# The down projection's accumulators move from SBUF to DRAM: ACT copies each finished tile out of PSUM and a DMA adds it to an array in DRAM

## The chip, the core and the metric

The kernel runs on one core of one Trainium2 chip. Each engine executes its own instructions in order: TensorE (PE) multiplies, VectorE (DVE) and ScalarE (ACT) do elementwise work and read PSUM, GpSimd (POOL) does elementwise work and can issue DMAs, SyncE (SP) issues most DMAs here. The metric is the device time of one execution in microseconds; lower is better.

## The reference, cut to what matters

The layer is a token-mixing block (attention heads beside a recurrent group) followed by an MLP. The change lies in the MLP alone, which is, for 512 tokens, D = 2048 and FF = 8192, all in float32:

```python
h = _rmsnorm(x, pre_mlp_g) * (1.0 + scale_m) + shift_m
y = jnp.square(jax.nn.relu(h @ w_up)) @ w_down
x = x + gate_m * _rmsnorm(y, post_mlp_g)
```

## The kernel before, in words

**Precision.** Each float32 operand is split into a high and a low part (`hl`: a CAST on ACT writes the high part, a TENSOR_TENSOR subtract on DVE the low part), and each product is three matmuls (high by high, high by low, low by high).

**Groups and rounds.** FF is cut into 16 groups of 512. While PE does the down projection of group g (steps "D"), it also does the up projection of group g+1 (steps "U"). The string `ROUND` writes this order out by hand: 22 steps, 14 of them D (12 matmuls each) and 8 U (24 matmuls each). There are 15 such rounds; `FIRST` is the order of the first. After them `down_last` does the down projection of the last group, token tile by token tile (128 tokens at a time), adds it to the sums, norms the row and stores it.

**Seven products.** The down projection of one group for one of two column sets c (512 columns of each half of D) is a Strassen-like scheme: seven products f = 0 to 6 instead of eight. Each writes a PSUM tile `dn` of 128 x 1024 (two token tiles by 512 columns). There are two such tiles, and f = 2, 3, 6 go on in the tile of f = 0, 1, 4. So a product can start only when the tile has been read that was written two products earlier. `product` (line 1194) issues the 12 matmuls (L1207 to L1209) and then adds the tile to its place: f = 0 and 5 to `V`, the other five to parts of `y`, an SBUF tile of 4 token tiles by 2048 columns (32 KB a partition). The addition is one DVE TENSOR_TENSOR (L1218); in the first group ACT copies instead where nothing is there yet (L1216). In the last round `add_V` (L1246) adds `V` to three parts of `y`.

**What orders the work.** The order on each engine is fixed when the program is built. `ahead` runs the weight preparation two steps ahead of PE. Weights come through SP's queue: `w_up` into `raw` tiles, `w_down` into `B` tiles (five of them, also used for `lraw`, the last group's `w_down`, and for `x2r`, the residual rows that `down_last` reads back). From the second round to the sixth, `interleave` adds one unit of the modulation's gate to each U step (its weights are read from `w_mod` through the same `raw` tiles). At the end of a round `hidden` (ACT's Relu into `u`, DVE's square) and `make_forms` (CASTs `fH`, subtracts `fL`) prepare the next group's operands.

Of the kernel before, what the change touches and what calls it, by code (L numbers as in the profile page):

```python
# [10 lines left out]
F32 = mybir.dt.float32  # L11
# [4 lines left out]
ALU = mybir.AluOpType  # L16
# [4 lines left out]
P = 128  # L21
S = 512
NT = S // P
D = 2048
# [28 lines left out]
def encoder_layer(ctx: ExitStack, tc: tile.TileContext, a, out):  # L53
    nc = tc.nc

    def pool(name, bufs=1, **kw):
        return tc.tile_pool(name=name, bufs=bufs, reuse_waits="tile", **kw)
# [18 lines left out]
    dram = ctx.enter_context(pool("dram", space=DRAM))  # L76
# [2 lines left out]
    w_mod, w_in, w_uq, w_ukv = a["w_mod"][0], a["w_in"][0], a["w_uq"][0], a["w_ukv"][0]  # L79
    w_out, w_up, w_down = a["w_out"][0], a["w_up"][0], a["w_down"][0]  # L80
    x2_d = dram.tile([S, D], F32, name="x2_d")

    def mmt(name):
        return banks["mm"].tile([P, 512], F32, tag="mm", name=name)
# [142 lines left out]
    def mm3(o, s_h, s_l, m_h, m_l, first, last):  # L227
        nc.tensor.matmul(o, s_h, m_h, start=first, stop=False)  # L228
        nc.tensor.matmul(o, s_h, m_l, start=False, stop=False)  # L229
        nc.tensor.matmul(o, s_l, m_h, start=False, stop=last)  # L230
# [5 lines left out]
    def rstd(r, ss, n):  # L236
        nc.scalar.activation(r, ss, AF.Sqrt, bias=eps[:, 0:1], scale=1.0 / n)
        nc.vector.reciprocal(r, r)
# [84 lines left out]
    with ExitStack() as ph:  # L323
# [385 lines left out]
        for gid, w, rate in ((("kv", 0), 256, RATE["kv"]), (("ql", 0), 512, RATE["ql"])):  # L709
            pss = run_block(gid, 0, KD, units, PER[gid[0]], steps, rate)  # L710
            if w == 256:
                t4 = v_tile()
                dst = [t4[:, t, :] for t in range(NT)]
            else:
                t2 = [z_tile(), z_tile()]
                dst = [t2[t // 2][:, t % 2, :] for t in range(NT)]
# [44 lines left out]
    for i in range(2):  # L761
        c = 2 * 2048 + 1024 * i
# [3 lines left out]
    with ExitStack() as ph:  # L766
# [66 lines left out]
        for k0 in range(0, 4, 2):  # L833
            src = w_uq[k0 * P:(k0 + 2) * P, :].rearrange("(k p) (h c) -> p k h c", p=P, c=192)
# [196 lines left out]

    with ExitStack() as ph:
        ml = ph.enter_context(pool("ml"))
        y = ml.tile([P, NT, D], F32, name="y")
        V = ml.tile([P, 2, 1024], F32, name="V")
        G = ml.tile([P, D], F32, name="G")
        NG = FF // 512
# [2 lines left out]
        def btile(name):  # L1040
            return ml.tile([P, 1024], F32, tag="B", name=name, bufs=NB)

        def ubank(n):
            return banks["up"].tile([P, 512], F32, tag="up", name=f"up{n}")

        def dset(name):
            return banks["dn"].tile([P, 1024], F32, tag="dn", name=name)
# [30 lines left out]
        for i in range(2):  # L1078
            c = 5 * 2048 + 1024 * i
# [114 lines left out]
        def product(q, fm, H, L):  # L1194
            s, f = divmod(q, 7)
            g, c = divmod(s, 2)
            fH, fL = fm[FORMS[f]]
            goes_on = {2: 0, 3: 1, 6: 4}.get(f)
            X = sets[f] = sets.pop(goes_on) if goes_on is not None else dset(f"dn{f}")
            for t in range(2):  # L1200
                o = X[:, 512 * t:512 * t + 512]
                ts_ = slice(t * P, (t + 1) * P)
                for k in range(2):
                    first, last = k == 0 and goes_on is None, k == 1
                    sh, sl, mh, ml_ = fH[:, k, ts_], fL[:, k, ts_], H[:, k, :], L[:, k, :]
                    skip = goes_on is not None
                    nc.tensor.matmul(o, sh, mh, start=first, stop=False, skip_group_check=skip)  # L1207
                    nc.tensor.matmul(o, sh, ml_, start=False, stop=False, skip_group_check=skip)  # L1208
                    nc.tensor.matmul(o, sl, mh, start=False, stop=last, skip_group_check=skip)  # L1209
            cs = slice(512 * c, 512 * c + 512)  # L1210
            c2 = slice(1024 + 512 * c, 1024 + 512 * c + 512)
            dst, fresh = [(V[:, :, cs], True), (y[:, 2:4, c2], True), (y[:, 0:2, cs], True), (y[:, 0:2, c2], True),
                          (y[:, 2:4, c2], False), (V[:, :, cs], False), (y[:, 2:4, cs], True)][f]
            Xv = X.rearrange("p (t n) -> p t n", t=2)
            if g == 0 and fresh:
                nc.scalar.copy(dst, Xv)  # L1216
            else:
                nc.vector.tensor_tensor(dst, dst, Xv, ALU.add)  # L1218


        VSIGN = {(0, 1): ALU.add, (2, 0): ALU.add, (2, 1): ALU.add}
        held = []

        def hold(g):
# [16 lines left out]
            return uu  # L1241

        def add_V(c, t0, t1, j):
            cs = slice(512 * c, 512 * c + 512)
            o = y[:, t0:t1, 1024 * j + 512 * c:1024 * j + 512 * c + 512]
            nc.vector.tensor_tensor(o, o, V[:, :, cs], VSIGN[t0, j])  # L1246

        def down_last(uu):
            for t in range(NT):
                ts_ = slice(t * P, (t + 1) * P)  # L1250
                xr = [btile(f"x2r{h}") for h in range(2)]
                for h in range(2):
                    nc.sync.dma_start(xr[h], x2_d[t * P:(t + 1) * P, 1024 * h:1024 * h + 1024])
                r = small.tile([P, 6], F32, tag="r6", name="r6")
                for c in range(4):
                    cs = slice(512 * c, 512 * c + 512)
                    ps = ubank(f"l{t}")
                    for k in range(4):
                        H, L = held[2 * c + k // 2]
                        mm3(ps, uu[k][0][:, ts_], uu[k][1][:, ts_], H[:, k % 2, :], L[:, k % 2, :], k == 0, k == 3)  # L1260
                    yv = y[:, t, cs]
                    nc.vector.tensor_tensor(yv, yv, ps, ALU.add)
                    jk = stream.tile([P, 1024], F32, tag="raw", name="yjk", bufs=4)[:, 0:512]
                    nc.scalar.activation(jk, yv, AF.Square, accum_out=r[:, 1 + c:2 + c])
                    nc.vector.tensor_tensor(yv, yv, G[:, cs], ALU.mult)
                nc.vector.reduce_sum(r[:, 0:1], r[:, 1:5], axis=AX.X)
                rstd(r[:, 0:1], r[:, 0:1], D)
                for c in range(4):
                    cs = slice(512 * c, 512 * c + 512)
                    nc.vector.scalar_tensor_tensor(y[:, t, cs], y[:, t, cs], r[:, 0:1],  # L1270
                                                   xr[c // 2][:, 512 * (c % 2):512 * (c % 2) + 512], ALU.mult, ALU.add)
                    nc.sync.dma_start(out[t * P:(t + 1) * P, cs], y[:, t, cs])


        pss = [mmt(f"up{n}") for n in range(4)]
# [26 lines left out]
        n = 0  # L1302
        for g in range(NG - 1):
            fm = make_forms(u if g == 0 else hidden(pss))
            pss = [ubank(i) for i in range(4)]
            for _ in range(22):
                ahead(n + 1 + LEAD)
                what, _, i = steps[n]
                H, L = wts.pop(n)
                if what == "U":  # L1310
                    up_mms(pss, i, H, L, 0, NT)
                    if g == NG - 2:
                        if i >= 8:
                            hold(NG - 1)
                        if i == KD - 2:
                            uu = last_forms(pss)
                    elif g > 0:
                        interleave(units, 1)
                else:
                    product(i, fm, H, L)  # L1320
                    if g == NG - 2:
                        c, f = divmod(i % 14, 7)
                        done[c].add(ORDER[f])
                        for need, t0, t1, j in (({5, 4}, 2, 4, 1), ({5, 3}, 0, 2, 1), ({5, 6}, 2, 4, 0)):
                            if need <= done[c] and (c, t0, j) not in added:
                                added.add((c, t0, j))
                                add_V(c, t0, t1, j)
                n += 1
        for _ in range(4):
            hold(NG - 1)  # L1330
        down_last(uu)


# [13 lines left out]
def build(nc, shapes):  # L1347
    aps = {n: nc.dram_tensor(f"in_{n}_dram", s, mybir.dt.from_np(np.dtype(d)), kind="ExternalInput").ap()
           for n, (s, d) in shapes.items()}
    out = nc.dram_tensor("out_0_dram", (1, S, D), F32, kind="ExternalOutput").ap()  # L1350
    with tile.TileContext(nc) as tc:
        encoder_layer(tc, aps, out[0])
# [12 lines left out]
```

## Time and profile before

| | us |
|---|---|
| runs of the kernel before | 2413.72, 2422.41, 2425.74 (median 2422.41) |
| profiled execution, its own time | 2417.74 |
| its span, first to last instruction | 2415.9 |
| granted TensorE clock, mean | 0.995 |
| busy: PE / DVE / ACT / POOL | 2340.0 / 1781.2 / 933.9 / 121.1 |
| DMA traffic of the span | 341.77 MB, mean 141 GB/s |

The table's busy times are sums over the whole span. The kernel has stages with different limits, so what matters for the change is read in the MLP's stage, about 1142 to 2416 us of the span. The span leaves out some 1.8 us that the profiled execution's time holds (2417.74 less 2415.9).

### The profile page before, as it was taken

To read this page: it belongs to the slowest core of one execution; us is meant where nothing else is said; L and a number is where in the kernel's file an instruction comes from. 1 tells how busy PE (TensorE), PEld (TensorE's weight loads), DVE (VectorE), ACT (ScalarE), POOL (GpSimd) and SP (SyncE) were. 2 spreads that over 40 slices of the span, in tenths; PEclk is the share of its full clock that TensorE was granted. 3 is DMA by queue.
4 is the path that set the end of the run, shared out by engine and by line. 5 is a ranking of instruction groups with operands and counts; after the bars stand their busy time and mean duration, and the time that the engine had idled before them with its cause. 6 is when DMAs were issued, how large, how long until landed. Compare 5 with 4: busy or idle time off the path is not lost.

```text
span 2415.9 us, 29649 instructions
## 1 busy us (share of the span) xinstructions
PE 2340.0 (97%) x11342; PEld 1944.6 (80%) x11342; DVE 1781.2 (74%) x2222; ACT 933.9 (39%) x1439; POOL 121.1 (5%) x127
## 2 busy tenths in 40 slices
PE   4999999999999999999999999999999999999998
PEld 3778888889977777879888888888888888888886
DVE  5984776767868765387688878876777678677777
ACT  5223334343444432375533333333333333333342
POOL 0111212121110000000000000000000000000000
PEclk9999999999999999999999999999999999999999
DMA  9873353535533246375445354433333333324234
GB/s 317 286 244 104 105 175 97 175 96 179 184 109 96 89 133 214 120 252 186 127 149 170 104 175 148 141 112 105 105 100 104 96 119 91 110 87 118 84 121 131
DMA packets 193801, 341.77 MB, mean 141 GB/s; under 512 B 16886, under 2 KB 65148, under 8 KB 192124
## 3 DMA queue, kind: packets, MB, share of 16 engines
q1 hardware_dynamic: 192464, 339.72, 45.0%
q8 instruction: 89, 1.46, 0.3%
q14 instruction: 52, 0.43, 0.1%
q10 hardware_dynamic: 1196, 0.16, 0.0%
HBM read 331.45 MB, written 8.39 MB: 141 GB/s over the span
## 4 chain that ended last, share of the span: by engine, by line
PE 66%; DVE 2%; DMA 1%; ACT 1%; issue 0%; DVEq 0%; ACTq 0%
PE up L230 10%; PE up L228 10%; PE up L229 10%; PE dn L1207 8%; PE dn L1209 8%; PE dn L1208 8%; PE wo L229 2%; PE wo L230 2%; PE wo L228 2%; PE pT L911 1%; PE upl L230 1%; PE upl L229 1%; PE upl L228 1%; PE sc L893 1%; DMA raw<-in_w_mod_dram 0%
## 5 line engine op out<-in xcount | busy, mean ns | idle before, releaser
L233 ACT CAST wH<-B 128x1024 fp32r<-128x1024 f32 x210 | 221.1, 1053 | 509.6 <-PE up L229 199.5
L234 DVE TENSOR_TENSOR wL<-B,wH 128x1024 fp32r<-128x1024 f32 x210 | 256.5, 1222 | 173.8 <-issue 68.9
L1207 PE MATMUL dn<-wH,fH 128*128 128x512 f32 x840 | 329.3, 392 | 1.3 <-DVE y L1218 1.3
L1209 PE MATMUL dn<-wH,fL 128*128 128x512 f32 x840 | 327.5, 390 | 0.0
L1208 PE MATMUL dn<-wL,fH 128*128 128x512 f32 x840 | 326.7, 389 | 0.0
L214 ACT CAST wH<-raw 128x512 fp32r<-128x512 f32 (+1 forms) x320 | 182.0, 611 | 334.3 <-PE wo L230 93.1
L215 DVE TENSOR_TENSOR wL<-raw,wH 128x512 fp32r<-128x512 f32 (+1 forms) x320 | 222.4, 725 | 117.4 <-issue 60.1
L271 DVE SCALAR_TENSOR_TENSOR modacc<-raw,cond,modacc 128x1024 f32<-128x1024 f32 x120 | 159.2, 1327 | 69.9 <-DMA raw<-in_w_mod_dram 69.4
L230 PE MATMUL up<-recH,wL 128*128 128x512 f32 (+1 forms) x544 | 207.9, 382 | 0.0
L228 PE MATMUL up<-recH,wH 128*128 128x512 f32 (+1 forms) x544 | 207.9, 382 | 0.0
L230 PE MATMUL up<-atH,wL 128*128 128x512 f32 (+1 forms) x544 | 204.6, 379 | 3.0 <-DVE wL L215 3.0
L229 PE MATMUL up<-recL,wH 128*128 128x512 f32 (+1 forms) x544 | 207.3, 381 | 0.0
L228 PE MATMUL up<-atH,wH 128*128 128x512 f32 (+1 forms) x544 | 205.1, 378 | 0.0
L229 PE MATMUL up<-atL,wH 128*128 128x512 f32 (+1 forms) x544 | 205.0, 378 | 0.0
L234 DVE TENSOR_TENSOR wL<-raw,wH 128x1024 fp32r<-128x1024 f32 x120 | 146.3, 1220 | 76.7 <-issue 51.6
L1207 PEld LDWEIGHTS dn<-wH,fH 128*128 128x128 f32 x840 | 157.6, 188 | 35.9 <-issue 1.7
L1209 PEld LDWEIGHTS dn<-wH,fL 128*128 128x128 f32 x840 | 157.6, 188 | 34.3
L1208 PEld LDWEIGHTS dn<-wL,fH 128*128 128x128 f32 x840 | 157.8, 188 | 33.9 <-issue 0.5
L233 ACT CAST wH<-raw 128x1024 fp32r<-128x1024 f32 x120 | 126.4, 1053 | 151.5 <-PE dn L1209 140.5
L1218 DVE TENSOR_TENSOR y<-y,dn 128x1024 f32<-128x1024 f32 x142 | 172.2, 1213 | 0.1
L230 PEld LDWEIGHTS up<-atH,wL 128*128 128x128 f32 x544 | 102.7, 190 | 21.8 <-DVE wL L215 3.2
L230 PEld LDWEIGHTS up<-recH,wL 128*128 128x128 f32 x544 | 102.0, 188 | 22.4
(369 smaller groups left out, 4661.2 us busy)
## 6 DMA issues: line engine op xcount, KB each, us to landing
raw<-in_w_up_dram SPq DMA_DIRECT2D x136, 512.0 KB, 3.7
raw<-in_w_mod_dram SPq DMA_DIRECT2D x128, 512.0 KB, 3.5
B<-in_w_down_dram SPq DMA_DIRECT2D x120, 512.0 KB, 4.2
raw<-in_w_in_dram SPq DMA_DIRECT2D x128, 256.0 KB, 3.1
mraw<-in_w_mod_dram SPq DMA_DIRECT2D x48, 512.0 KB, 5.4
raw<-in_w_out_dram SPq DMA_DIRECT2D x40, 512.0 KB, 4.6
raw<-in_w_in_dram SPq DMA_DIRECT2D x24, 512.0 KB, 4.9
mraw<-in_w_mod_dram SPq DMA_DIRECT2D x32, 256.0 KB, 4.1
```

The source lines that it names most:

```text
L214: nc.scalar.copy(H[:, o], raw[:, o])
L215: nc.vector.tensor_tensor(L[:, o], raw[:, o], H[:, o].bitcast(F32), ALU.subtract)
L228: nc.tensor.matmul(o, s_h, m_h, start=first, stop=False)
L229: nc.tensor.matmul(o, s_h, m_l, start=False, stop=False)
L230: nc.tensor.matmul(o, s_l, m_h, start=False, stop=last)
L233: nc.scalar.copy(h_out, src)
L234: nc.vector.tensor_tensor(l_out, src, h_out.bitcast(F32), ALU.subtract)
L271: nc.vector.scalar_tensor_tensor(st["acc"][:, :w], v[:, k, :], cond[:, kt:kt + 1], st["acc"][:, :w], ALU.mult, ALU.add)
L1207: nc.tensor.matmul(o, sh, mh, start=first, stop=False, skip_group_check=skip)
L1208: nc.tensor.matmul(o, sh, ml_, start=False, stop=False, skip_group_check=skip)
L1209: nc.tensor.matmul(o, sl, mh, start=False, stop=last, skip_group_check=skip)
L1218: nc.vector.tensor_tensor(dst, dst, Xv, ALU.add)
```

## The change

`y` is no longer in SBUF. For each pair of token tiles t, half j and column set c there is an array `y_d[t, j, c]` of 256 x 512 in DRAM, eight in all. For the five products whose result went to `y`, ACT copies the PSUM tile into an SBUF tile `st` (four buffers), and POOL issues a DMA of 512 KB that adds `st` to `y_d` (`accum_op`), or writes it where nothing is there yet. `V` stays in SBUF and is still added to on DVE. `add_V` becomes such a DMA too, from `V`. `down_last` reads `y_d` back, four DMAs of 256 KB for each token tile, into `yt` (two buffers), and goes on as before.

```diff
+    y_d = {(t, j, c): dram.tile([2 * P, 512], F32, name=f"y_d{t}{j}{c}")
+           for t in (0, 2) for j in range(2) for c in range(2)}
...
-        y = ml.tile([P, NT, D], F32, name="y")
...
-            cs = slice(512 * c, 512 * c + 512)
-            c2 = slice(1024 + 512 * c, 1024 + 512 * c + 512)
-            dst, fresh = [(V[:, :, cs], True), (y[:, 2:4, c2], True), (y[:, 0:2, cs], True), (y[:, 0:2, c2], True),
-                          (y[:, 2:4, c2], False), (V[:, :, cs], False), (y[:, 2:4, cs], True)][f]
             Xv = X.rearrange("p (t n) -> p t n", t=2)
-            if g == 0 and fresh:
-                nc.scalar.copy(dst, Xv)
+            if f in (0, 5):
+                dst = V[:, :, 512 * c:512 * c + 512]
+                if g == 0 and f == 0:
+                    nc.scalar.copy(dst, Xv)
+                else:
+                    nc.vector.tensor_tensor(dst, dst, Xv, ALU.add)
             else:
-                nc.vector.tensor_tensor(dst, dst, Xv, ALU.add)
+                t, j = {1: (2, 1), 2: (0, 0), 3: (0, 1), 4: (2, 1), 6: (2, 0)}[f]
+                st = ml.tile([P, 1024], F32, tag="st", name="st", bufs=4)
+                nc.scalar.copy(st, X)
+                add_y(t, j, c, st.rearrange("p (t n) -> p t n", t=2), g == 0 and f != 4)
+
+        def add_y(t, j, c, src, fresh=False):
+            dst = y_d[t, j, c].rearrange("(t p) n -> p t n", p=P)
+            if fresh:
+                nc.gpsimd.dma_start(dst, src)
+            else:
+                nc.gpsimd.dma_start(dst, src, accum_op=ALU.add)
...
         def add_V(c, t0, t1, j):
-            cs = slice(512 * c, 512 * c + 512)
-            o = y[:, t0:t1, 1024 * j + 512 * c:1024 * j + 512 * c + 512]
-            nc.vector.tensor_tensor(o, o, V[:, :, cs], VSIGN[t0, j])
+            add_y(t0, j, c, V[:, :, 512 * c:512 * c + 512])
...
         def down_last(uu):
             for t in range(NT):
+                yt = ml.tile([P, D], F32, tag="yt", name="yt", bufs=2)
+                for c in range(4):
+                    nc.sync.dma_start(yt[:, 512 * c:512 * c + 512],
+                                      y_d[t // 2 * 2, c // 2, c % 2][t % 2 * P:t % 2 * P + P, :])
...
-                    yv = y[:, t, cs]
+                    yv = yt[:, cs]
```

**ACT at the end of a round.** These are ACT's rows where the last round but one ends, before the change. `up_…` are the four PSUM tiles of the up projection, `B_…` and `raw` weights.

```order
L1118 ACTIVATE u<-up_16852 128x512
L233 CAST fH<-u 128x512
L233 CAST wH<-B_17002 128x1024
L1118 ACTIVATE u<-up_16853 128x512
L233 CAST fH<-u 128x512
L233 CAST wH<-raw 128x1024
L233 CAST wH<-B_17188 128x1024
L233 CAST wH<-raw 128x1024
L233 CAST fH<-u 128x512
```

The same place after the change; the three copies empty the PSUM tiles of f = 3, f = 4 and f = 6.

```order
L1119 ACTIVATE u<-up_17119 128x512
L235 CAST fH<-u 128x512
L235 CAST wH<-B_17273 128x1024
L1119 ACTIVATE u<-up_17120 128x512
L235 CAST fH<-u 128x512
L1221 COPY st<-dn_17471 128x1024
L235 CAST wH<-raw 128x1024
L1221 COPY st<-dn_17596 128x1024
L235 CAST wH<-B_17465 128x1024
L235 CAST wH<-raw 128x1024
L235 CAST fH<-u 128x512
L1221 COPY st<-dn_17596 128x1024
```

The copies stand between the CASTs, in ACT's order; each waits for its product on PE and for a free `st`, and the CASTs behind it wait with it.

**POOL at the end of the last round.** POOL's queue has no row in the MLP before the change. After it, its last rows are these; `y_d_76` is `y_d[0, 1, 1]`, `y_d_78` is `y_d[2, 0, 1]` and `y_d_80` is `y_d[2, 1, 1]`.

```order
L1229 DMA y_d_76<-st 128x2x512
L1229 DMA y_d_80<-st 128x2x512
L1229 DMA y_d_76<-V 128x2x512
L1229 DMA y_d_80<-V 128x2x512
L1229 DMA y_d_78<-st 128x2x512
L1229 DMA y_d_78<-V 128x2x512
```

Each adds to an array to which an earlier row of the queue adds, and waits until that one has landed.

**SP at the end.** Before the change SP's last rows hold the last group's weights, the residual rows and the stores.

```order
L1228 DMA lraw<-in_w_down_dram 128x2x512 x8
L1253 DMA x2r_17960<-x_d 128x1024
L1253 DMA x2r_17961<-x_d 128x1024
L1253 DMA x2r_18044<-x_d 128x1024
L1253 DMA x2r_18045<-x_d 128x1024
L1253 DMA x2r_18128<-x_d 128x1024
L1272 DMA out_dram<-y 128x512 x4
```

After it the reads of `y_d` stand among them (`y_d_73` to `y_d_76` belong to token tiles 0 and 1, `y_d_77` to tiles 2 and 3).

```order
L1261 DMA yt<-y_d_73 128x512 x2
L1153 DMA B_17846<-in_w_down_dram 128x2x512
L1153 DMA B_17868<-in_w_down_dram 128x2x512
L1238 DMA lraw<-in_w_down_dram 128x2x512 x2
L1261 DMA yt<-y_d_75 128x512 x2
L1238 DMA lraw<-in_w_down_dram 128x2x512 x6
...
L1265 DMA x2r_18450<-x_d 128x1024
L1261 DMA yt<-y_d_76 128x512 x2
L1284 DMA out_dram<-yt 128x512 x4
L1265 DMA x2r_18451<-x_d 128x1024
L1265 DMA x2r_18539<-x_d 128x1024
L1261 DMA yt<-y_d_77 128x512
```

The reads for tiles 0 and 1 are issued ahead of, and among, the last group's weights. Those for tile 2 stand behind the stores of tile 0, whose `yt` they take over.

## Rows read from the trace of the kernel before

**Rows 1.** The page, part 1: busy us (share of the span) and instructions.

```profile
PE 2340.0 (97%) x11342; PEld 1944.6 (80%) x11342; DVE 1781.2 (74%) x2222; ACT 933.9 (39%) x1439; POOL 121.1 (5%) x127
```

**Rows 2.** Windows: a round with gate units, a late round, the last round, the tail.

```profile
core 0: us, PE busy (x) PEld busy (x) DVE busy (x) ACT busy (x) POOL busy (x), PEclk, DMA share, GB/s
1225.30:1307.70 82.40, 82.40 (x362) 67.53 (x361) 68.50 (x65) 29.31 (x33) 0.00 (x0) 1.00 0.48 147
...
2184.80:2267.20 82.40, 82.40 (x361) 67.54 (x360) 60.32 (x58) 29.31 (x33) 0.00 (x0) 1.00 0.35 103
2295.00:2363.50 68.50, 67.22 (x294) 54.70 (x293) 54.23 (x49) 27.71 (x31) 0.00 (x0) 1.00 0.40 125
2363.50:2407.00 43.50, 43.06 (x187) 34.68 (x185) 33.46 (x54) 11.41 (x33) 0.00 (x0) 1.00 0.41 129
2407.00:2416.00 9.00, 0.00 (x0) 0.00 (x0) 3.95 (x8) 1.02 (x3) 0.00 (x0) 0.74 0.35 117
```

**Rows 3.** Tile `dn`: ns min/median/max of one, first and last start, shapes.

```profile
L1218 DVE TENSOR_TENSOR y<-y,dn x142: 1208/1212/1222, 1168.7 to 2365.9; 128x1024 f32<-128x1024 f32 x142
...
L1216 ACT COPY y<-dn x8: 1010/1017/1019, 1148.3 to 1203.8; 128x1024 f32<-128x1024 f32 x8
```

**Rows 4.** DMA issues of the span: count, KB each, median us to landing.

```profile
B<-in_w_down_dram SPq DMA_DIRECT2D x120, 512.0 KB, 4.2
...
x_d<-mix SPq DMA_DIRECT2D x4, 1024.0 KB, 4.5
...
out_dram<-y SPq DMA_DIRECT2D x16, 256.0 KB, 2.7
```

**Rows 5.** Line 1152, SP's issue of a 512 KB load: ns min/median/max.

```profile
L1152 SPq DMA_DIRECT2D B<-in_w_down_dram x120: 367/368/472, 1100.6 to 2306.7; - x120
```

**Rows 6.** Timeline of PE at a round's end: f3, f4, f5, f6, next U begin.

```profile
2267.25 0.40 PE L1207 MATMUL dn<-wH,fH 128*128 128x512 f32 x1
...
2270.00 0.39 PE L1207 MATMUL dn<-wH,fH 128*128 128x512 f32 x1
...
2272.72 0.40 PE L1207 MATMUL dn<-wH,fH 128*128 128x512 f32 x1
...
2275.46 0.39 PE L1207 MATMUL dn<-wH,fH 128*128 128x512 f32 x1
...
2278.18 0.39 PE L228 MATMUL up<-atH,wH 128*128 128x512 f32 x1
```

**Rows 7.** Timeline of DVE there: the additions of f3 and f4.

```profile
2271.21 1.21 DVE L1218 TENSOR_TENSOR y<-y,dn 128x1024 f32<-128x1024 f32 x1
...
2272.94 1.21 DVE L1218 TENSOR_TENSOR y<-y,dn 128x1024 f32<-128x1024 f32 x1
```

**Rows 8.** Timeline of ACT there.

```profile
2270.19 0.62 ACT L233 CAST fH<-u 128x512 fp32r<-128x512 f32 x1 [1.43 <-DVE u L1120]
2270.71 1.05 ACT L233 CAST wH<-raw 128x1024 fp32r<-128x1024 f32 x1
2272.92 1.05 ACT L233 CAST wH<-B 128x1024 fp32r<-128x1024 f32 x1 [1.16 <-PE dn L1209]
```

**Rows 9.** Timeline of PE in the last round: the one stall.

```profile
2356.50 0.39 PE L228 MATMUL upl<-atH,fH 128*128 128x512 f32 x1
2358.17 0.47 PE L1207 MATMUL dn<-wH,fH 128*128 128x512 f32 x1 [1.28 <-DVE y L1218]
```

**Rows 10.** Timeline of DVE at the end: last `V`, then three additions of `down_last`.

```profile
2361.35 1.21 DVE L1218 TENSOR_TENSOR V<-V,dn 128x1024 f32<-128x1024 f32 x1
...
2373.36 0.69 DVE L1262 TENSOR_TENSOR y<-y,upl 128x512 f32<-128x512 f32 x1 [0.63 <-PE upl L230]
...
2389.95 1.28 DVE L1262 TENSOR_TENSOR y<-y,upl 128x512 f32<-128x512 f32 x2
```

**Rows 11.** Timeline of SP at the end: stores of token tile 0.

```profile
2376.94 2.32 SPq L1272 DMA_DIRECT2D out_dram<-y  x4
```

More of the change, by code (lines that the diff above doesn't have):

```diff
@@ L1209, in product @@
                     nc.tensor.matmul(o, sl, mh, start=False, stop=last, skip_group_check=skip)
-            cs = slice(512 * c, 512 * c + 512)
-            c2 = slice(1024 + 512 * c, 1024 + 512 * c + 512)
-            dst, fresh = [(V[:, :, cs], True), (y[:, 2:4, c2], True), (y[:, 0:2, cs], True), (y[:, 0:2, c2], True),
-                          (y[:, 2:4, c2], False), (V[:, :, cs], False), (y[:, 2:4, cs], True)][f]
             Xv = X.rearrange("p (t n) -> p t n", t=2)
-            if g == 0 and fresh:
-                nc.scalar.copy(dst, Xv)
-            else:
-                nc.vector.tensor_tensor(dst, dst, Xv, ALU.add)
-        VSIGN = {(0, 1): ALU.add, (2, 0): ALU.add, (2, 1): ALU.add}
+            if f in (0, 5):
[4 more added lines that the diff above has]
+                    nc.vector.tensor_tensor(dst, dst, Xv, ALU.add)
+            else:
+                t, j = {1: (2, 1), 2: (0, 0), 3: (0, 1), 4: (2, 1), 6: (2, 0)}[f]
[8 more added lines that the diff above has]
+                nc.gpsimd.dma_start(dst, src, accum_op=ALU.add)
         held = []
@@ L1269, in down_last @@
                     cs = slice(512 * c, 512 * c + 512)
-                    nc.vector.scalar_tensor_tensor(y[:, t, cs], y[:, t, cs], r[:, 0:1],
+                    nc.vector.scalar_tensor_tensor(yt[:, cs], yt[:, cs], r[:, 0:1],
                                                    xr[c // 2][:, 512 * (c % 2):512 * (c % 2) + 512], ALU.mult, ALU.add)
-                    nc.sync.dma_start(out[t * P:(t + 1) * P, cs], y[:, t, cs])
+                    nc.sync.dma_start(out[t * P:(t + 1) * P, cs], yt[:, cs])
         pss = [mmt(f"up{n}") for n in range(4)]
```

## Prediction, written before the changed kernel was run

> **What bounds the kernel now.** I began with the page's busy times. PE is busy 97% of the span, DVE 74%, ACT 39% [rows 1]. That is an average over stages, so I cut the stage that the change touches into rounds [rows 2]. The reader is to see that in a whole round PE is busy 82.40 of 82.40 us, while DVE is busy 60 to 69 us and ACT 29 us. In the last round PE lacks 1.3 us (67.22 of 68.50), and in the tail 0.4 us. So PE alone sets the length of this stage; what DVE does there counts only where PE waits for it. The timeline has one such place: in the last round a matmul of f = 5 waits 1.28 us for the addition of f = 3 on DVE [rows 9]. After the last matmul some 9 us remain (2407 to 2416), in which the last token tile is normed and stored; the change leaves these operations as they are.
>
> **What is removed.** 142 additions of 1.213 us on DVE [rows 3] make 172 us, ten in a usual round, or 12.1 us. DVE falls from 60.3 to about 48 us in a late round. PE does not wait for DVE in these rounds, so this is worth nothing there. Six `add_V` additions of the same shape go too; most stand beside PE's work. All that removal can gain is the stall of 1.28 us.
>
> **What ACT gains.** 150 copies of a PSUM tile of 128 x 1024, ten a round. The trace has eight of the same shape, 1.017 us each [rows 3]. ACT goes from 29.3 to about 39.5 us of 82.4 [rows 2]. The place to check is the end of a round, where four products follow each other and the same PSUM tile comes up again after one step. f = 5 begins at 2272.72 and f = 6 at 2275.46 [rows 6]. Before, the addition of f = 3 ended at 2272.42 (2271.21 + 1.21), 0.3 us ahead of need [rows 7]. After, ACT's order has the copy of f = 3 behind the CAST `fH`, which ended at 2270.81 [rows 8]; f = 4 begins at 2270.00, so f = 3 has ended then but for its pipeline. The copy runs from about 2270.8 to 2271.8, 0.9 us ahead of need. The copy of f = 4 waits for that product's end, about 2272.9, and ends at 2273.9, 1.5 us ahead of need. The CASTs behind it (`wH`, 2272.92 before) move back by about 1 us; they prepare weights two steps ahead, so the next U step at 2278.18 and the D step behind it cover that. If this cover went, each round would cost what the copy is late; I take nothing.
>
> **What POOL and the DMA engines gain.** POOL has nothing to do in the MLP before (0.00 us in every round) [rows 2]. It now issues 156 transfers of 512 KB, ten a round: one for each 8.24 us. The trace holds no DMA issued from POOL and none that adds, so I bound both.
>
> *Time to landing.* Writes of 256 KB land in 2.7 us and of 1024 KB in 4.5 us [rows 4], which puts 512 KB at about 3.3 us (a third of the way): the lower end, if the addition costs nothing. Upper end: two loads of 512 KB (4.2 us each) and a write, one behind another, 11.7 us. I take a load and a write, 7.5 us, as the adding transfer must at least read its destination before it writes it. What waits for a landing is spaced wider than that. `st` comes round every four copies; in the tightest stretch, from f = 1 of the second column set to f = 6 at the round's end, that is two U steps and five D steps. A D step takes 2.73 us (2270.00 to 2272.72, [rows 6]), a U step has twice the matmuls, so 24.6 us. f = 4 adds to the array of f = 1, about 19 us later. Neither is reached at 7.5 us or 11.7 us as long as transfers overlap.
>
> *DMA engines' share.* In a late round a share of 0.35 moves 103 GB/s [rows 2], so all 16 engines together would move 294 GB/s, and 512 KB take 1.78 us of all of them. Bounds: once (1.78 us) and three times (source, destination, write: 5.35 us). I take two, 3.56 us: reads bind, and there are two of them. Ten a round add 0.22 to 0.65 to the share, 0.43 as taken. A late round then stands at 0.78 (0.57 to 1.00), a round with gate units at 0.91 (0.70 to 1.13). Weights come later but are asked for well ahead; PE is not touched while the share stays below 1.
>
> The page on the reads: the Trainium skill (Collectives: The Full Stack, "The bandwidth ceiling: the fold count and why AG ≠ RS ≠ AR") says that an addition inside a DMA engine is not slow by itself but needs two reads where a copy needs one, which halved the rate measured there. By that the price is 3.56 us and the sum the same; by three passes a gate round would be over full. No run here shows either yet.
>
> *Issue on POOL.* The nearest row is SP's, 0.37 us [rows 5]. It is a different queue, so I take it as the lower end only. The upper end that matters is 8.24 us a transfer: below it POOL keeps up.
>
> **The tail.** Token tiles 0 and 1 need `V`'s last value. DVE adds it at 2361.35 to 2362.56 [rows 10]; a transfer of 7.5 us lands at 2370.1; the read of 256 KB, at the price of a write of that size (2.7 us), at 2372.8. Its first use is the fourth addition of tile 0, 2373.36 before: 0.6 us to spare. At 11.7 us it would be 3.6 us late. PE fills four PSUM banks ahead, and DVE is idle 10 us in the tail (33.46 of 43.50, [rows 2]), so most of that would be made up. Reads for tile 2 wait for the stores of tile 0: issued until 2379.3 [rows 11], landed by 2382, read back by 2384.7, used at 2389.95. SP's queue also carries reads of `y_d` ahead of the last group's weights; they delay these only where a transfer takes far longer than taken here. I take 0 for the tail, bounds -1.3 (the stall goes) and +4.
>
> **The sum.** Loop 0, tail 0: 2417.7 us on the profiled execution's own time. That lies 4.7 us below the median of the runs, so the forecast in their terms is 2422 us, no change.
>
> **Rivals.**
> *1. The DMA engines fill up in the rounds with gate units.* For it: share 0.48 there already [rows 2], and three passes give 1.13. Against: two passes give 0.91. It decides from (1 - 0.48) x 82.4 / 10 = 4.3 us of all engines a transfer. At 1.13, five rounds grow by 13%, 5 x 82.4 x 0.13 = 54 us: 2476 us. Weights would come late and ACT's CASTs would wait for DMA.
> *2. The transfers go one at a time, and slowly.* If POOL's issue or the engines take one adding transfer after another, each in d us, the loop follows them from d = 8.24 us on. ACT's copy then waits for a free `st`, the CASTs wait behind it, and PE waits for its PSUM tile. At the upper end, 11.7 us, it costs 150 x (11.7 - 8.24) = 519 us: 2941 us. For it: no row shows POOL issuing anything. Against: 7.5 us is below the threshold even without any overlap. The Trainium skill (SBUF — State Buffer, "Who interferes with whom") says that a DMA issued from GpSimd stalls while DVE holds the port pair that both share, which its two-port modes do, and that TENSOR_TENSOR has no such mode; DVE's additions and splits here are TENSOR_TENSOR, so by that rule this rival gains little, and no run here shows it.
> *3. DVE's relief shows.* For it: 172 us less on an engine busy 74%. Against: PE busy in full in every whole round. At most 1.3 us: 2421 us, not to be told from no change.
>
> **How the numbers follow.** Two kernels here can be told apart from about 0.5%, 12 us. No change (2410 to 2434): 0.68, with the tail's bounds and rival 3 inside. Rival 1: 0.13. Rival 2: 0.15. Faster by over 0.5%: 0.04, for something that I do not see. The likeliest is 2422 us. The range leaves out rival 2 and the rare gain, 0.19 in all: 2410 to 2480, with the upper end just above rival 1's price. Slower is 0.13 + 0.15 = 0.28.
>
> **What would show it.** Right: PE still busy in the whole of each round; DVE down by about 12 us and ACT up by about 10 us a round; DMA share 0.7 to 0.85 in late rounds; copies that wait for PE and not for a DMA; an adding transfer landing in 5 to 9 us. Wrong: `COPY st` waiting for a `y_d` transfer, or POOL's queue issuing without pause (rival 2); CASTs `wH` waiting for `raw` or `B` in the gate rounds (rival 1); DVE's first addition of a token tile waiting for `yt` (tail).

## Result and the profile after

| | us |
|---|---|
| kernel before, median of 4 runs | 2420.11 (2413.72 to 2425.74) |
| changed kernel, median of 4 runs | 2458.78 (2456.13 to 2461.7) |
| ratio | 1.0158, 95% interval 1.0136 to 1.0181 |
| profiled execution: span before, after | 2415.9, 2455.6 |

The change makes the kernel slower by 39 us. The forecast was no change, at 2422 us; the time lies in the range given (2410 to 2480), but not for a reason that the likeliest case held.

The page's part 1 of the changed kernel, which answers to [rows 1]:

```profile
PE 2351.1 (96%) x11342; PEld 1951.1 (79%) x11342; DVE 1618.6 (66%) x2074; ACT 1058.5 (43%) x1581; POOL 305.4 (12%) x283
```

DVE lost 163 us and ACT gained 125 us. PE issues the same 11342 matmuls, but they took 11 us more. Where the other 28 us are, the windows show. The columns are those of [rows 2]: a round with gate units, a late round, and then slices of the last round and the tail.

```profile
1225.30:1307.70 82.40, 82.40 (x362) 67.55 (x361) 58.07 (x56) 38.00 (x44) 11.87 (x10) 1.00 0.86 214
2185.00:2267.20 82.20, 82.20 (x361) 67.41 (x360) 49.20 (x48) 38.10 (x43) 12.08 (x10) 1.00 0.81 168
...
2320.00:2340.00 20.00, 19.13 (x82) 14.97 (x81) 10.00 (x9) 5.84 (x6) 3.63 (x3) 1.00 0.76 154
2340.00:2360.00 20.00, 8.10 (x27) 5.81 (x27) 5.76 (x5) 3.85 (x4) 3.00 (x3) 0.73 0.68 151
2360.00:2380.00 20.00, 15.27 (x58) 11.75 (x57) 12.87 (x14) 14.51 (x19) 2.31 (x3) 0.84 0.76 176
2380.00:2400.00 20.00, 20.00 (x81) 16.14 (x81) 7.66 (x10) 3.21 (x8) 3.14 (x3) 0.92 0.73 192
```

The reader is to see two things. In the whole rounds PE is still busy in full, and the shares of the DMA engines are those forecast (0.81 late, 0.86 with gate units, where 0.78 and 0.91 were reckoned). So the loop lost nothing. All of the loss but a later start of some 2 us lies behind 2320 us. There PE waits, and the granted clock, 1.00 in every round, falls to 0.73 in the slice of the long wait and is 0.84 and 0.92 in the next two: part of these slices ran at the lower of the two levels (1.2 GHz for 2.4). In the last slice shown 81 matmuls take 20.00 us, 0.247 us each; in the late round 361 take 82.20, 0.228 each.

PE's waits from 1142 us to the end (total, times, longest); before there was one, of 1.3 us [rows 9]:

```profile
PE dn L1208 <- DVE V L1217: 11.6, 1, 11.6
PE upl L230 <- DVE yt L1274: 7.5, 3, 3.1
PE dn L1208 <- ACT st L1221: 2.7, 1, 2.7
PE upl L230 <- ACT fH L235: 2.0, 1, 2.0
PE dn L1209 <- DVE wL L236: 1.0, 2, 0.8
```

They add up to 24.8 us. The account of the 39.7 us between the two spans: PE waits 23.5 us longer; its matmuls take 11 us longer after the waits (from 2320 to 2443 us 377 of them are busy for 97.97 us; at the 85.28 us for 369 of the same stretch before, they would take 87.1); from the last matmul to the end it is 12.3 us where it was 9.3, 3 us. That is 37.5 us; the rest, some 2 us, is a later start of the stage.

**The wait of 11.6 us, followed back.** PE's product waits for DVE's addition to `V`, but DVE had been waiting itself. ACT's timeline in the last round shows for what (start, duration, instruction, in brackets the idle time before it and what ended it):

```profile
2335.77 1.05 ACT L235 CAST wH<-B 128x1024 fp32r<-128x1024 f32 x1
2352.69 1.04 ACT L235 CAST atH<-lraw 128x1024 fp32r<-128x1024 f32 x1 [15.87 <-DMA lraw<-in_w_down_dram]
```

ACT's next instruction is a CAST of `lraw`, the last group's weights, and they are not there. Behind that CAST stand the copies and the weights of the round. DVE waits for the CAST with its subtract, and the addition to `V` stands behind that:

```profile
2353.77 1.23 DVE L236 TENSOR_TENSOR atL<-lraw,atH 128x1024 fp32r<-128x1024 f32 x1 [15.18 <-ACT atH L235]
2354.91 1.22 DVE L1217 TENSOR_TENSOR V<-V,dn 128x1024 f32<-128x1024 f32 x1
```

SP's timeline shows why the weights are late (start, length of the group, count):

```profile
2316.55 11.78 SPq L1238 DMA_DIRECT2D lraw<-in_w_down_dram  x2
2343.09 0.82 SPq L1261 DMA_DIRECT2D yt<-y_d  x2
2344.01 26.18 SPq L1238 DMA_DIRECT2D lraw<-in_w_down_dram  x6
```

Between the second and the third load of `lraw` stand two reads of `y_d` (the row `yt<-y_d_75` of the order shown above). SP stood at the first of them from 2328.33 until 2343.09, for a transfer that adds `V` to that array. All its waits of this kind in this stage are `L1261 <- DMA y_d<-V` 48.5 us (3 times, this one 14.8, the longest 21.6) and `L1261 <- DMA y_d<-st` 19.9 us. POOL's timeline shows why that transfer is late:

```profile
2306.95 1.21 POOL L1229 DMA_DIRECT2D y_d<-st  x1 [7.89 <-issue]
2313.53 1.20 POOL L1229 DMA_DIRECT2D y_d<-st  x1 [5.37 <-issue]
2323.75 1.21 POOL L1229 DMA_DIRECT2D y_d<-st  x1 [9.01 <-issue]
2330.73 1.20 POOL L1229 DMA_DIRECT2D y_d<-V  x1 [5.77 <-DVE B L1167]
2337.05 1.21 POOL L1229 DMA_DIRECT2D y_d<-V  x1 [5.12 <-issue]
2343.39 1.20 POOL L1229 DMA_DIRECT2D y_d<-st  x1 [5.13 <-issue]
...
2422.67 1.21 POOL L1229 DMA_DIRECT2D y_d<-V  x1 [9.38 <-DMA y_d<-st]
```

The idle time between them ends, in most rows, on nothing that the profile names ("issue"). The times to landing name it. The transfers that start at 2306.95 and 2313.53 landed after 6.3 and 9.9 us, at 2313.2 and 2323.4:

```profile
DMA to landing us min/median/max: 6.3/6.3/6.3
...
DMA to landing us min/median/max: 9.9/9.9/9.9
```

The next ones start at 2313.53 and 2323.75, 0.32 us later each. So it is in the whole stage. Of the 145 times that one adding transfer follows another, the second never starts earlier than 0.317 us after the first has landed, and 104 times it starts just then, whatever the profile names as the end of the wait. Adding transfers go one at a time, each for its landing and 0.32 us more; the closest two start 5.9 us apart.

The values of `V` that the read waits for had been ready since 2320.4 (DVE's addition ends there). The second of the two transfers from `V` is the one to `y_d_75`, as SP's row shows: it starts at 2337.05 and has landed at 2343.1, when SP goes on. The last round has 16 transfers where a usual round has 10. The last of them starts at 2422.67, 16 us after the time at which PE had finished in the kernel before (2406.6). So the tail's reads are late as well.

The transfers themselves, taken singly, were as forecast. All instructions on `st` from 1142 to 2320 us (ns min/median/max, first and last start), what POOL waited for before them, and the time to landing:

```profile
L1221 ACT COPY st<-dn x144: 1002/1017/1022, 1150.0 to 2315.5; 128x1024 f32<-128x1024 f32 x144
L1229 POOL DMA_DIRECT2D y_d<-st x135: 1194/1204/1428, 1170.9 to 2313.5; - x135
L1227 POOL DMA_DIRECT2D y_d<-st x8: 725/738/931, 1151.3 to 1207.2; - x8
...
  issue: 399.6, 55
...
DMA to landing us min/median/max: 4.5/7.8/11.5
```

7.8 us to landing where 7.5 was taken, 1.017 us a copy as in [rows 3]. An adding transfer's issue takes POOL 1.204 us, a plain one 0.738 (L1227); SP's load took 0.368 [rows 5].

### The profile page after: what moved, and what is told of

The parts are those of the page before. It is cut to its first block, busy times and chain, and to the rows that moved or that the text cites. A ratio compares the mean times of both kernels' runs of the same rounds, so it can differ in the third digit from the quotient of the medians.

```text
span 2455.6 us, 29973 instructions
## 1 busy us (share of the span) xinstructions
PE 2351.1 (96%) x11342; PEld 1951.1 (79%) x11342; DVE 1618.6 (66%) x2074; ACT 1058.5 (43%) x1581; POOL 305.4 (12%) x283
## 3 DMA queue, kind: packets, MB, share of 16 engines
q0 software_dynamic: 41408, 81.80, 21.4%
## 4 chain that ended last, share of the span: by engine, by line
PE 62%; DMA 3%; issue 3%; DVE 2%; ACT 1%; POOL 0%; SPq 0%; DVEq 0%; POOLq 0%; ACTq 0%
PE up L232 9%; PE up L230 9%; PE up L231 9%; PE dn L1208 8%; PE dn L1210 7%; PE dn L1209 7%; PE wo L230 2%; PE wo L231 2%; PE wo L232 2%; DMA lraw<-in_w_down_dram 1%; DMA y_d<-st 1%; DMA raw<-in_w_mod_dram 1%; PE pT L913 1%; PE sc L895 1%; DVE wL L217 1%
## 5 line engine op out<-in xcount | busy, mean ns | idle before, releaser
L1208 PE MATMUL dn<-wH,fH 128*128 128x512 f32 x840 | 331.2, 394 | 14.4 <-DVE V L1217 11.6
L1229 POOL DMA_DIRECT2D y_d<-st x142 | 171.8, 1210 | 1013.2 <-ACT st L1221 435.2
L1221 ACT COPY st<-dn 128x1024 f32<-128x1024 f32 x150 | 152.2, 1016 | 165.1 <-PE dn L1210 165.1
```

Of the source, the lines that this page charges most:

```text
L1229: nc.gpsimd.dma_start(dst, src, accum_op=ALU.add)
```

## Experiments

Each kernel is the changed kernel with the edit shown. "Before" is the kernel before on the same chip: 2417.49 us for e1 to e4, 2417.82 for e5 to e8, 2417.23 for e9 and e10. Two theories: **Q**, the loss comes from queues that stand in order behind late transfers (SP's behind reads of `y_d`, the tail's behind POOL's); **L**, the work itself is the loss (copies on ACT, the DMA engines' load).

**e1: nothing waits for `y_d`.** The tail reads rows of the layer's input in its place, so the output lacks the sums.

```diff
-                                      y_d[t // 2 * 2, c // 2, c % 2][t % 2 * P:t % 2 * P + P, :])
+                                      x_d[t * P:t * P + P, 512 * c:512 * c + 512])
```

> The tail reads yt from the input x instead of y_d, so SP's reads wait for no adding transfer; the 156 transfers, the ACT copies and their traffic all stay (the sums of the down projection are left out of the output). Theory Q (queue): the loss is SP's reads waiting for y_d and holding the last group's weights behind them, so 2415 to 2425 us and no PE stall over 2 us in the last round. Rival L (load): the extra DMA traffic and ACT's copies slow the end by themselves, so 2440 us or more.

2426.78 us, 1.0038 [1.0026, 1.0049]; 1.8 us above Q's figure, so a narrow miss, and far from L's. All 156 transfers are still made, one at a time as before, and of 39 us over the kernel before 9 are left. SP issues the eight loads of `lraw` from 2314.56 to 2349.04 without a read among them; in the changed kernel the last of them is issued at 2370.19, 21 us later. In the last round PE's two waits are 2.7 (Q had none over 2) and 1.3 us, the tail's 43 us from 2364 are busy in full. What is left at the end is the program's own wait for the last transfer from `V`, issued at 2419.08: `SPq L1363 <- DMA y_d<-V`, 4.2 us; from the last matmul to the end it is 16.2 us. L falls as the main cause; Q is left.

**e2: the reads behind the weights.** A copy of one column of the last `lraw` to `yt` makes the reads of tiles 0 and 1 wait for it.

```diff
+                if t < 2:
+                    for c in range(4):
+                        nc.vector.tensor_copy(yt[:, 512 * c:512 * c + 1], held[7][1][:, 1, 511:512].bitcast(F32))
```

> The reads of y_d for token tiles 0 and 1 are made to stand behind all eight lraw loads in SP's queue (a one-column copy on DVE from the last split weights writes yt first). Theory Q: the PE stalls of 12 and 12 to 15 us in the last round go; what stays is the tail waiting for the last adding transfers, since POOL issues them 6.3 us apart at best and the last round has 16: 2425 to 2440 us. Rival L: 2445 us or more.

2449.83 us, 1.0134 [1.0119, 1.0149]: a miss, and by the time alone it lies where L was put; the trace says otherwise. The long wait is gone, as meant (PE busy 39.34 of 44 us from 2320 to 2364), but 32 of the 39 us are still there. SP's longest wait and PE's moved into the tail:

```profile
SPq L1264 <- DMA y_d<-V: 32.8, 2, 19.7
...
PE upl L230 <- DVE yt L1277: 17.9, 2, 11.9
```

The place of the reads decides where PE stands; it does little for the time at which the transfers are done: the last is issued at 2412.75, 10 us earlier than in the changed kernel. e7 puts 19 us of what is left on the transfers from `V`.

**e3: more memory for descriptors.** The kernel is built with 1024 B a partition for the descriptors of POOL's DMAs; this has 1792.

```diff
-    nc = bacc.Bacc("TRN2", target_bir_lowering=False, num_devices=1, dynamic_dma_scratch_size=1024)
+    nc = bacc.Bacc("TRN2", target_bir_lowering=False, num_devices=1, dynamic_dma_scratch_size=1792)
```

> The memory for descriptors of POOL's transfers is 1792 instead of 1024 bytes a partition, nothing else. Theory R: POOL's unexplained waits of 5 us between issues are waits for room for descriptors, so back-to-back issues come under 5 us apart, the reads of y_d wait half as long, and the time falls to 2425 to 2445 us. Rival S: adding transfers go one at a time for another reason; the spacing stays at 6.3 us and the time at 2455 to 2462 us.

2434.54 us, 1.0071 [1.0048, 1.0095], within what was expected: of 39 us over the kernel before 17 are left. POOL's timeline of the same stretch:

```profile
2308.46 1.19 POOL L1229 DMA_DIRECT2D y_d<-st  x1 [6.97 <-ACT st L1221]
2316.62 1.20 POOL L1229 DMA_DIRECT2D y_d<-st  x1 [6.96 <-ACT st L1221]
2325.10 2.42 POOL L1229 DMA_DIRECT2D y_d<-V  x2 [7.28 <-DMA y_d<-st]
2330.89 1.21 POOL L1229 DMA_DIRECT2D y_d<-st  x1 [3.37 <-ACT st L1221]
...
2391.61 1.19 POOL L1229 DMA_DIRECT2D y_d<-V  x1 [8.07 <-DMA y_d<-st]
```

The two transfers from `V` now follow each other in 1.2 us. No idle time on POOL ends on "issue" any more (435.0 us in 61 places in the changed kernel); each transfer waits for its copy, or for the transfer before it to the same array. In this kernel 67 of the same 145 start before the one ahead of them has landed, and up to three are under way at once; in the changed kernel never two. So it was the descriptors' room that made them go one at a time. They pay for it with a longer landing, 8.4 us in the mean from 1225 to 2278 us where it was 7.7. The Trainium skill (DMA: Bandwidth & Descriptors, "SWDGE vs HWDGE vs iDMA") says that a DMA issued from GpSimd has its descriptors written to rings in an area of SBUF, and that adding is to be had on this path alone; what happens when the area is small it doesn't say, and this pair of runs shows it.

**e4: the same transfers without the addition.** The sums are not formed.

```diff
-                nc.gpsimd.dma_start(dst, src, accum_op=ALU.add)
+                nc.gpsimd.dma_start(dst, src)
```

> All 156 transfers write y_d and none adds (so y_d holds only the last product); same queues, same order. Theory Q with the addition as the cost: a write lands in 3 to 4 us and is issued some 2.5 us after the one before, as in the first group; POOL has no backlog, 2418 to 2430 us. Rival: the software-issued transfer itself is slow, spacing about 6 us, 2450 us or more.

2422.61 us, 1.0022 [1.0013, 1.0032]. The software queue of the whole span (packets, MB, share of 16 engines), in the changed kernel and here:

```profile
q0 software_dynamic: 41408, 81.80, 21.4%
```

```profile
q0 software_dynamic: 22464, 81.80, 9.0%
```

For the same bytes the addition takes nearly twice the packets and 2.4 times the engines' time: 9.0% of 2422.8 us over 156 transfers is 1.40 us of all engines for a plain one, which lands in 5.8 us (3 to 4 were expected); 21.4% of 2455.6 us, less eight plain ones of the first group, is 3.48 us for each of the other 148. In the same way a plain one has 144 packets and an adding one 272. Plain transfers are not held apart even with 1024 B ("issue" 0.2 us in all, and 46 of the 145 start before the one ahead has landed), which fits their having about half the packets. SP's queue has its reads where the changed kernel has them, and still only 5 of 39 us are left: standing ahead of the weights costs little once the transfers are not late.

**e5: `V` added on DVE, with e3's memory.** `add_V` sends nothing; `down_last` adds `V` after the read.

```diff
-            add_y(t0, j, c, V[:, :, 512 * c:512 * c + 512])
+            pass
...
+                    if (t // 2, c // 2) != (0, 0):
+                        nc.vector.tensor_tensor(yv, yv, V[:, t % 2, 512 * (c % 2):512 * (c % 2) + 512], ALU.add)
```

> Edit: descriptor memory 1792 B a partition, as in e3, and V's six additions no longer go through DRAM: down_last adds V to the rows it has read, on DVE (12 additions of 128 x 512). Theory Q (what is lost is SP's queue standing behind reads that wait for the chain of adding transfers): the chain of each array is one transfer shorter, the last one lands at about 2374 us; no read of the last round waits over 5 us, the stall for lraw goes, and the time is 2418 to 2428 us, within 0.5% of before. Theory L (the adding transfers themselves are too slow in the last round, whatever waits for them): the e3 loss of 17 us stays, 2432 us or more.

2436.24 us, 1.0076 [1.0061, 1.0091]: a miss, no better than e3, and by the time alone where L was put. The last transfer is issued at 2371.63, 20 us earlier than in e3, but DVE's timeline shows a new wait:

```profile
2367.48 1.22 DVE L1217 TENSOR_TENSOR V<-V,dn 128x1024 f32<-128x1024 f32 x1 [1.55 <-PE dn L1210]
2382.51 1.29 DVE L1275 TENSOR_TENSOR yt<-yt,V 128x512 f32<-128x512 f32 x2 [13.80 <-DMA yt<-y_d]
```

In this program's order the additions of `V` to the last columns of tile 0 stand ahead of DVE's first addition of PE's results, so the whole tail waits for one read, which waits for a transfer that was issued at 2363.15 together with another and landed 13.6 us later. DVE has taken SP's part: an engine that stands in order at a late read. The figure for Q had left it out. But that this one transfer landed so late, among four loads of `x2r`, looks like load, and in so far like L; no run separates the two.

**e6: e2 and e3 together.** Diff: both of the above.

> Edit: both halves at once, the descriptor memory of e3 and the reads behind the last group's weights of e2. If the two are separate prices (the reads' place costs the stall in the last round, the spacing of the transfers costs the tail), the last round has no stall over 3 us and the tail waits only for the chain f6, then V: 2426 to 2438 us. If they are one and the same price, it is no better than e3, 2434 us.

2430.08 us, 1.0056 [1.0041, 1.0071], in the range for two separate prices; by its time it can't be told from e3, whose interval overlaps, and PE's waits are much the same (7.3 us in all, 9.1 in e3, none over 2.7 in either). So with the larger memory the place of the reads is worth little, and two separate prices are not shown. In the tail DVE waits 7.0 us for the first read, which is issued only at 2369.74, behind the weights, and is there 7.3 us later; and 4.7 us for the read behind the chain of f = 3, then `V`, to one array.

**e7: e2 and e5's addition, with 1024 B.**

> Edit: descriptor memory as in the changed kernel (1024), reads behind the last group's weights as in e2, V added on DVE from SBUF as in e5. If the six transfers from V are what makes the tail late, four of them queued one behind another at 6.3 us at the end, then the last transfer is issued some 20 us earlier and the time is 2420 to 2432 us, against 2450 in e2. If the spacing of 6.3 us alone makes the tail late, it stays above 2440 us.

2430.97 us, 1.0056 [1.0041, 1.0071], as expected. POOL's last rows are still held apart ("issue"), but there are few left:

```profile
2361.35 1.21 POOL L1229 DMA_DIRECT2D y_d<-st  x1 [8.46 <-ACT st L1221]
2370.21 1.20 POOL L1229 DMA_DIRECT2D y_d<-st  x1 [7.65 <-issue]
2380.90 1.21 POOL L1229 DMA_DIRECT2D y_d<-st  x1 [9.48 <-issue]
```

The last one starts at 2380.90, 32 us earlier than in e2. So with the small memory it was the six transfers from `V`, queued among the last twelve, that carried the backlog into the tail: against e2 they are worth 19 us.

**e8: two `st` buffers.** `bufs=4` becomes `bufs=2`.

> Edit: two st buffers in place of four. The prediction held that a landing of 7.5 us is hidden because st comes round only every four copies (24.6 us in the tightest stretch). With two buffers the tightest stretch is f4 to f6 at a round's end, about 5.5 us, less than a landing: each round's last copies should wait for a transfer and PE for its PSUM tile, 3 to 10 us a round, 45 to 150 us in all: 2500 to 2610 us. If the time stays within 10 us of 2459, the copies had far more room than was reckoned.

2459.40 us, 1.0171 [1.0154, 1.0188]: a miss, the same as the changed kernel. From 1250 to 2320 us ACT's copies do wait for transfers now, but PE hardly does:

```profile
ACT st L1221 <- DMA y_d<-st: 47.5, 20, 5.2
...
PE dn L1208 <- ACT st L1221: 1.0, 2, 0.7
```

They take 2.4 us in the mean. From 1142 to 2320 us PE is busy 1173.9 of 1178 us where it was 1178.0 with four buffers, so these waits cost 4 us at most. The four buffers had far more room than they needed; in the changed kernel no copy of these rounds waits for a transfer.

**e9: e3, e5 and e2 together.**

> Edit: e3, e5 and the order of e2 together: descriptor memory 1792, V added from SBUF on DVE, the reads of y_d behind the last group's weights. If the three causes (spacing of the transfers, the V transfers at the end of the chain, the reads ahead of the weights) account for the loss, what is left is the late copy of f3 (two waits of PE of 2.7 and 2 us where before had one of 1.3) and at most one short wait for a read: 2420 to 2428 us, and no DVE wait for yt over 6 us. If something else costs as well, it stays at 2430 us as e6 and e7.

2428.75 us, 1.0048 [1.0034, 1.0062]: 0.75 us above the bound given, so a narrow miss, and the wait for `yt` was longer too:

```profile
DVE yt L1279 <- DMA yt<-y_d: 10.2, 1, 10.2
```

The last matmul ends at 2411.0, 4.4 us later than in the kernel before (2406.6). Then it is 15.5 us to the end instead of 9.3: DVE starts the tail 10 us late, has 12 additions more in it, and runs behind PE to the end. The read that it waits for is issued at 2362.05; it stands with seven more reads, behind five loads of `x2r` and beside three adding transfers. The landing of these reads, where those of the changed kernel have a median of 2.9 us:

```profile
DMA to landing us min/median/max: 8.3/8.7/12.8
```

By its time e9 can't be told from e6 and e7.

**e10: copies and plain transfers alone.** e1 and e4 together.

> Edit: e1 and e4 together: every transfer writes and none adds, and the tail reads rows of the input's copy in DRAM in place of y_d, so nothing waits for a transfer; the sums are not formed. What is left of the change is ACT's copies, DVE's relief and plain transfers. By the waits seen in e1 and e4 (PE 2.7 and 1.3 to 1.9 us in the last round, 1.3 before) it is 3 us above before: 2418 to 2424 us. If DVE's relief were worth anything, it would be below before: 2415 us or less.

2421.22 us, 1.0016 [1.0007, 1.0025]. With no read of the sums and no addition, the change costs 4 us, and DVE's relief gives nothing. PE's waits in the last round:

```profile
PE dn L1208 <- ACT st L1221: 2.7, 1, 2.7
...
PE upl L230 <- ACT fH L235: 0.2, 1, 0.2
```

ACT's timeline of e4 shows the first: the copies of f = 3 and f = 4 stand behind the five CASTs of the three rows above them.

```profile
2357.55 1.17 ACT L235 CAST fH<-u 128x512 fp32r<-128x512 f32 x2
2358.59 1.07 ACT L235 CAST recH<-lraw 128x1024 fp32r<-128x1024 f32 x1
2359.54 1.17 ACT L235 CAST fH<-u 128x512 fp32r<-128x512 f32 x2
2360.58 1.95 ACT L1221 COPY st<-dn 128x1024 f32<-128x1024 f32 x2
```

No kernel here is faster than the kernel before.

| | reads wait for `y_d` | reads behind weights | room, B | `V` by | ratio |
|---|---|---|---|---|---|
| changed | yes | no | 1024 | DMA | 1.0158 |
| e2 | yes | yes | 1024 | DMA | 1.0134 |
| e3 | yes | no | 1792 | DMA | 1.0071 |
| e5 | yes | no | 1792 | DVE | 1.0076 |
| e6 | yes | yes | 1792 | DMA | 1.0056 |
| e7 | yes | yes | 1024 | DVE | 1.0056 |
| e9 | yes | yes | 1792 | DVE | 1.0048 |
| e1 | no | no | 1024 | DMA | 1.0038 |
| e4 | yes | no | 1024 | DMA, plain | 1.0022 |
| e10 | no | no | 1024 | DMA, plain | 1.0016 |

The intervals of e3, e5, e6, e7 and e9 overlap, each with each of the others: what is said to set these five apart rests on their traces, not on their times. The intervals of the changed kernel and of e3, of e2 and of e7, and of the changed kernel and of e1 or e4 do not overlap.

## Why the prediction was wrong, step by step

**Right: the loop.** PE stayed the bound in every whole round. DVE fell by 11 us a round (60.32 to 49.20), ACT rose by 9, the DMA shares and the landing came out as taken. 3.48 us of all engines for a transfer stands beside the 3.56 reckoned, and 7.8 us to landing beside 7.5, but both agree partly by luck: a plain transfer took 1.40 us of the engines where 1.78 was reckoned, and landed in 5.8 us where 3.3 was (e4). The two reads that the Trainium skill (Collectives: The Full Stack, "The bandwidth ceiling: the fold count and why AG ≠ RS ≠ AR") names fit the packets, 272 for 144; the engines' time, 2.5 times a plain one's, lies between two passes and three, and no run decides it. Rival 1 did not happen. Rival 3's 1.3 us did not show either (e10). That the loop kept up was close: a transfer took 7.67 us to landing in the mean from 1225 to 2278 us and 0.32 more, 8.0 us against the 8.24 that a round has for it.

**Right, but for the last round: ACT's copies.** At a usual round's end they stood as worked out: f = 3's copy from 2272.46, f = 4's from 2274.66, and PE never waited. In the last round four more CASTs (`recH`) stand among these rows, and f = 3's copy made PE wait 2.7 us. The bounds given for the tail, -1.3 to +4, had taken this cover for granted there too; e10 gives its price with all else that is left, 4 us.

**Wrong: that transfers overlap, and that their rate need only hold on the mean.** The times for `st` and for the array of f = 1 were said to be safe "as long as transfers overlap". They don't overlap: each adding transfer starts when the one before has landed. That is rival 2's mechanism, which the trace of before could not show. The prediction set it aside because 7.5 us is below 8.24 "even without any overlap", and "below it POOL keeps up". This holds over a round of ten, by 0.26 us a transfer. But transfers come in bursts, and the last round has 16 in the same 82 us, one for each 5.1 us; at 8.0 us each they fall behind, and what waits for them waits too. Rival 2's signs did not show it either: no copy waited for a transfer, and POOL's own issue stayed short (1.19 to 1.43 us in all 142); the time was in the landings between. e3 lets them overlap, and 22 of the 39 us are gone.

**Wrong: the sentence on SP's queue in the tail.** Reads of `y_d` ahead of the last group's weights were to "delay these only where a transfer takes far longer than taken here". A transfer took 7.8 us, as taken, and yet the reads held the weights back until 2344 us. What counts is when the awaited one is issued, behind all others: its `V` was ready at 2320.4, and it went at 2337.05, where with more room (e3) it went at 2326.3. And a read waits for all of the additions to its array, so the chain copy, transfer, `V`'s transfer, read is added up. The tail's sum took one transfer of 7.5 us from `V`'s last value to its landing. In the changed kernel `V`'s last value is there at 2385.3; its transfer for token tiles 0 and 1 goes at 2398.23, behind others, and has landed at 2404.27, 18.9 us after the value. A sign like the one named for the tail came: DVE's fourth addition of tile 0, not its first, waits 10.2 us for `yt`.

**Not foreseen: the clock.** 11 of the 39 us are matmuls at the lower clock in and after the waits. A wait of 11.6 us on PE cost nearly twice its length, if all of this is put down to it; no run here separates the two.

**Still open.** With all three repairs (e9) 11.5 us are left, of which e10 explains 4. The others lie in the tail, where DVE waits 10.2 us for the first read. That this read is late because it is issued behind the weights and lands among much other traffic is argued from its row; no run takes the traffic away and leaves the sums. How far it could be taken back by another order of DVE's work wasn't tried. Nor does any run show why 1024 B hold just one adding transfer; that the number of packets decides it is argued from e4.

## What to carry to other kernels

A transfer that is hidden on the mean is still late in the burst: where a result goes out and comes back through DRAM, follow the last ones in order, with each queue's waiting instruction and what stands behind it. Read when each transfer lands, too: a pause that ends on nothing can be the landing of the one before. A read that depends on a late write doesn't belong on a queue ahead of loads that others need. Before adding on the way to DRAM, look at the room for descriptors: 768 B a partition more let up to three transfers be under way here, and took away 22 of 39 us.

## What the runs showed of the hardware

An adding transfer of 512 KB issued from POOL costs 1.204 us of POOL (0.725 us for a plain one in e4), lands in 7.8 us (5.8 plain) and takes 3.48 us of all 16 DMA engines (1.40 plain). With 1024 B a partition for descriptors each starts at the earliest 0.317 us after the one before has landed; with 1792 B two follow in 1.2 us or less, and up to three are under way (e3). Of two issued together in e5, among four loads of `x2r`, the awaited one landed after 13.6 us. Loads of 512 KB by SP's queue slowed beside them: `B` lands in 6.0 us where it was 4.2 [rows 4], without effect on PE.
